# Attention's reciprocal row sums: to DRAM through a TensorE transpose, or straight from the 128x4 tile in 4-byte pieces

## The chip, the cores and the metric

The kernel runs on one core of a Trainium2 chip. The metric is the device time of one execution in microseconds (us); the time of a kernel is the median of its runs. Beside the times there is one profiled execution, from which all views are taken. A core has five engines that run their own instruction streams and wait for each other by semaphores: TensorE (PE, matrix multiply; its weight loads are shown apart as PEld), VectorE (DVE), ScalarE (ACT), GpSimd (POOL) and SyncE (SP). In this kernel SP issues every DMA, in the order of its own stream. SBUF is the on-chip memory with 128 partitions, PSUM holds TensorE's results in 8 banks, and DRAM is the chip's main memory.

## The reference

One inference step of a two-layer encoder, for a prompt of 1024 tokens and 8 samples of 16 tokens (1152 rows of width 1024), all in 4-byte floats. Each layer is attention with 16 heads of width 64, then a gated feed-forward network of width 2816 with a short causal convolution; each half is closed by a layer norm. Layer 0 attends to the own chunk of 64 and the 2 chunks before it, with a learned sink in the softmax; layer 1 to the own chunk and the 8 before it. What matters here is the softmax:

```
s = q . k * scale + bias           # per head, masked to the band
m = max(s)                         # layer 0: max(s.max, sink)
e = exp(s - m)
p = e / (e.sum + exp(sink - m))    # layer 1: p = e / e.sum
o = p . v
```

The division by the row sum can be made on `p` or, after the second product, on `o`; the kernel does it on `o`.

## The kernel before, in words

The stages follow each other: projections of the modulation vectors (`ada`), attention of layer 0 ("A" here), its output projection, feed-forward, attention of layer 1 ("B"), its output projection, feed-forward. Matmuls are run in split precision: each operand is a high and a low part, held in two tiles, and three products are added. The modulation weights of later stages are streamed in and multiplied in the background of attention A (`ada`, L209 loads and L211 matmuls).

Inside an attention, `work` is a list of 64 pairs: 8 column blocks `c` (two heads each), 2 heads `a`, 4 groups `g` of 256 queries. For each pair, in this order, there are

- `scores` (L507, L510 matmuls, softmax at L473 on DVE and L477 on ACT): unnormalised exponentials `p` with queries on the partitions, and their row sum into one column of the tile `L`, one column for each 128 queries; in A the row's maximum goes to `M`;
- `weigh`, one pair later: TensorE transposes of `p` (L533), evacuated by ACT and DVE (L538, L539);
- `values`, three pairs later in A and two in B: the second product (L552) and its evacuation into `on` (L563, L564), with head width on the partitions and queries along the row.

After every second pair, `sums` takes the four new columns of `L`: 128 partitions (queries) by 4 (query tiles). In A it adds the sink (L573, L574). It takes reciprocals (L575). The factor is needed along the row, for all 64 partitions of a head, since `on` has its queries there. So the four columns are turned into four rows by a TensorE transpose into a PSUM bank (L577, from the two banks `tbk` that `weigh` uses too), DVE copies them to the tile `rl` (L578), and a DMA writes 4 rows of 128 numbers, 512 bytes each, to the DRAM array `rD` (L580). When the values of both pairs are there, `normalise` reads the 512 numbers back with one DMA that repeats them on 64 partitions (L586, into `rb`), multiplies `on` by them (L589, on POOL, the very last one on DVE), and stores the result to DRAM (`oN`, L591), from where it is loaded for the output projection (`oload`, L597). The last column block stays in SBUF. `rb` has one place for each of the two heads `a`.

Beside this, small items handle the samples; they end in stores of 128 partitions by 4 by 16 numbers into `oSD` in B (L695). Loads of keys and values for the next head pair are at L436 and L437, of the bias at L485, of weights at L166, of the output projection's rows and constants at L806, L807, L811 and L907.

The Python order is a draft. A scheduler runs through it with estimated durations and decides the final order of every engine's stream, SP's DMAs among them; a change of one step moves others. Semaphores are derived from what reads and writes what; DMAs share eight completion semaphores in turn, so that a DMA also waits for the one that used its semaphore before.

Of the kernel before, what the change touches and what calls it, by code (L numbers as in the profile page):

```python
# [88 lines left out]
class Trunk:  # L89
# [249 lines left out]
    def attention(self, l, wk):  # L339
        nc, I = self.nc, self.I  # L340
# [32 lines left out]
        sa, sc = (fa, fa) if l == 0 else (Arena(self.adaT[:, 0:720]), Arena(self.cT))  # L373
        pTs = sa.take(384)
        osm = sc.take(128)
        rl = sc.take(128)
        L = sa.take(128)
        M = sa.take(128) if l == 0 else None
        ost = sa.ring(1, 512) if l == 0 else sa.ring(2, 64)
# [2 lines left out]
        tbk = Ring(TB[l])  # L382
# [35 lines left out]
        for p in range(2):  # L418
            t = sb.next()[:, 0:KS]
# [148 lines left out]
        def sums(x):  # L568

            hh = 2 * x.head.c + x.head.a  # L570
            cs = slice(hh * 8 + 2 * x.g - 2, hh * 8 + 2 * x.g + 2)
            if l == 0:
                nc.scalar.activation(M[:, cs], M[:, cs], AF.Exp, bias=self.sinkH[:, hh : hh + 1])  # L573
                nc.vector.tensor_add(L[:, cs], L[:, cs], M[:, cs])  # L574
            nc.vector.reciprocal(L[:, cs], L[:, cs])  # L575
            t = self.bank(tbk.next())
            nc.tensor.transpose(t[0:4, 0:128], L[:, cs], self.ident)  # L577
            nc.vector.tensor_copy(rl[0:4, :], t[0:4, 0:128])  # L578
            q0 = (x.g // 2) * 512
            nc.sync.dma_start(self.rD[l][hh, q0 : q0 + 512].rearrange("(g q) -> g q", q=128), rl[0:4, :])  # L580

        def normalise(c, a, h):
            r = slice(64 * a, 64 * a + 64)
# [145 lines left out]
        for i, x in enumerate(work):  # L729
            scores(x)  # L730
            if i and work[i - 1].g % 2:
                sums(work[i - 1])
            for c, bi in QAT.get(i, ()):
                if bi is None:
                    qload(c)
                else:
                    qblock(c, bi, qw[c])
            if i >= lw:
                weigh(work[i - lw])
            if i >= lag:  # L740
                finish(i - lag)
            self.step(BGA)
            if not self.bg and len(sbk.items) == 4:
                sbk.items = [0, 1, 2, 3, 4]
            for _ in range(ITEMS.count(i)):
                steps += items.pop(0)
            for _ in range(min(len(steps), 1 + (len(steps) > 4) + (len(steps) > 8))):
                steps.pop(0)()
            for c in OAT.get(i, ()):
                oload(c)  # L750
        assert not items
        for f in steps:
            f()
        sums(work[-1])
        for i in range(len(work) - lw, len(work)):
            weigh(work[i])
# [582 lines left out]
```

## Time and profile before

| | us |
|---|---|
| median of 3 runs | 2995.66 |
| lowest and highest | 2993.42, 2997.04 |
| the profiled execution | 2989.15 |
| its span, first to last instruction | 2987.3 |

The mean granted TensorE clock of the profiled execution is 0.984 of full speed. Attention A takes about 120 to 410 us of the span, attention B about 1665 to 2012 us, by the first and last instruction of `sums`. In the views, a group's row gives line, engine, operation, tiles and shapes, count, then busy time and mean length of one in ns, then the idle time of the engine before them and what ended it. "PE PS L577" means an instruction of line 577 on PE that writes PSUM. PEq, SPq and the like are the engines' sequencers, which issue DMAs and wait for semaphores. Lines are those of the kernel before.

### The profile page before, as it was taken

What the parts mean: (1) busy time and instruction counts of PE and PEld (TensorE: products, weight loads), DVE (VectorE), ACT (ScalarE), POOL (GpSimd) and SP (SyncE); (2) the same over time, 40 slices, a digit from 0 to 9 for tenths busy, and PEclk for the clock granted to TensorE, in tenths of its full rate; (3) what the DMA queues carried; (4) which work ended last, traced back from release to release, by engine and by line L of the source; (5) the groups of instructions that cost most, each with busy time, mean ns of one, the idle gap of its engine ahead of it and who ended that gap; (6) DMA issues with size and microseconds to landing.
All of it is one profiled execution on the core that took longest, in us unless ns stands there. A gap on an engine that the chain in (4) does not pass through costs nothing.

```text
span 2987.3 us, 43224 instructions
## 1 busy us (share of the span) xinstructions
PE 2863.8 (96%) x16582; PEld 2545.5 (85%) x16582; DVE 1537.3 (51%) x3416; ACT 1145.7 (38%) x2432; POOL 908.0 (30%) x661
## 2 busy tenths in 40 slices
PE   7999889999999999999999999989999999999996
PEld 4886668888888898997999888867899999999995
DVE  4365668424444343358412677766724444444468
ACT  3464643332222222224434666662442222222224
POOL 2122332322222222344561121231432222222253
PEclk9999989999999999999999999999999999999998
DMA  8655353722222222212795467673311111111121
GB/s 299 189 150 160 109 151 113 238 81 77 94 81 86 83 72 99 82 64 103 267 309 165 130 152 195 181 226 118 125 50 38 41 43 46 43 41 40 42 84 74
DMA packets 175535, 353.95 MB, mean 118 GB/s; under 512 B 34632, under 2 KB 91784, under 8 KB 174944
## 3 DMA queue, kind: packets, MB, share of 16 engines
q1 hardware_dynamic: 175328, 351.19, 37.0%
q8 instruction: 130, 2.13, 0.3%
q14 instruction: 77, 0.63, 0.1%
HBM read 285.22 MB, written 75.35 MB: 121 GB/s over the span
## 4 chain that ended last, share of the span: by engine, by line
PE 79%; DVE 8%; DMA 6%; ACT 3%; POOL 2%; issue 2%; SPq 0%; DVEq 0%; ACTq 0%; POOLq 0%
PE PS L267 46%; PE PS L1050 16%; PE PS L279 8%; PE PS L552 2%; PE PS L211 2%; PE PS L533 2%; DMA ws<-in_wo_dram 1%; PE PS L507 1%; DMA F<-in_adaw_dram 1%; DVE F L473 1%; PE PS L510 1%; DMA F<-xd 1%; DVE acc L1110 1%; DMA ws<-oN 1%; POOL wl L162 1%
## 5 line engine op out<-in xcount | busy, mean ns | idle before, releaser
L267 PE MATMUL PS<-H,wh 128*128 128x384 f32 (+1 forms) x5472 | 1045.9, 339 | 0.3 <-DVE H L162 0.3
L267 PEld LDWEIGHTS PS<-H,wh 128*128 128x128 f32 x5472 | 966.6, 188 | 17.5 <-issue 7.5
L162 POOL TENSOR_TENSOR wl<-ws,wh 128x1024 fp32r<-128x1024 f32 x167 | 404.8, 2429 | 751.1 <-ACT wh L151 704.0
L979 DVE SCALAR_TENSOR_TENSOR F<-PS,F 128x256 f32<-128x256 f32 (+2 forms) x704 | 352.9, 512 | 535.7 <-ACT F L976 522.5
L267 PE MATMUL PS<-H,wl 128*128 128x384 f32 (+1 forms) x2736 | 565.1, 343 | 19.6 <-POOL wl L162 7.8
L267 PEld LDWEIGHTS PS<-H,wl 128*128 128x128 f32 x2736 | 486.3, 189 | 53.2 <-issue 18.6
L976 ACT ACTIVATE F<-PS,F 128x384 f32<-128x384 f32 x264 | 177.3, 672 | 751.1 <-PE PS L267 749.6
L1050 PE MATMUL PS<-wh,X 128*128 128x512 f32 x1320 | 412.2, 394 | 10.3 <-DVE acc L1041 4.1
L1041 DVE TENSOR_TENSOR acc<-acc,PS 128x512 f32<-128x512 f32 x324 | 221.4, 685 | 271.6 <-PE PS L1050 271.1
L1025 POOL TENSOR_TENSOR F<-F 128x384 f32<-128x384 f32 x132 | 138.0, 1046 | 649.4 <-ACT F L1023 647.5
L1050 PEld LDWEIGHTS PS<-wh,X 128*128 128x128 f32 x1320 | 245.4, 188 | 64.0 <-issue 6.7
L151 ACT CAST wh<-ws 128x1024 fp32r<-128x1024 f32 x174 | 180.0, 1045 | 154.9 <-PE PS L1050 75.3
L1050 PE MATMUL PS<-wl,X 128*128 128x512 f32 x660 | 216.4, 392 | 0.0
L279 PE MATMUL PS<-wh,H 128*128 128x256 f32 (+1 forms) x936 | 172.5, 314 | 6.3 <-DVE H L162 6.0
L279 PEld LDWEIGHTS PS<-wh,H 128*128 128x128 f32 x936 | 137.3, 195 | 17.0 <-DVE H L162 6.8
L1050 PEld LDWEIGHTS PS<-wl,X 128*128 128x128 f32 x660 | 124.1, 188 | 28.1
L589 POOL TENSOR_TENSOR F<-F,x2att 64x512 f32<-64x512 f32 x62 | 79.4, 1280 | 212.8 <-DVE F L564 171.4
L162 DVE TENSOR_TENSOR X<-F,X 128x384 fp32r<-128x384 f32 x110 | 96.9, 881 | 88.7 <-ACT X L151 88.4
L279 PE MATMUL PS<-x1att,H 128*128 128x512 f32 x504 | 131.8, 402 | 4.9 <-ACT x1att L151 2.7
L533 PE MATMUL PS<-C,F 128*128 128x128 f32 x720 | 118.3, 285 | 17.4 <-DVE wh L539 7.5
L1023 ACT ACTIVATE F<-F 128x384 f32<-128x384 f32 x132 | 69.2, 524 | 143.3 <-DVE F L979 129.0
L279 PEld LDWEIGHTS PS<-x1att,H 128*128 128x128 f32 x504 | 94.7, 190 | 27.8 <-ACT x1att L151 3.4
(211 smaller groups left out, 3477.8 us busy)
## 6 DMA issues: line engine op xcount, KB each, us to landing
ws<-in_wup_dram SPq DMA_DIRECT2D x88, 512.0 KB
F<-in_adaw_dram SPq DMA_DIRECT2D x74, 512.0 KB
ws<-in_wdn_dram SPq DMA_DIRECT2D x44, 512.0 KB
ws<-in_adaw_dram SPq DMA_DIRECT2D x32, 512.0 KB
x1att<-kH SPq DMA_DIRECT2D x60, 256.0 KB
xd<-F SPq DMA_DIRECT2D x27, 512.0 KB
F<-xd SPq DMA_DIRECT2D x27, 512.0 KB
vH<-X SPq DMA_DIRECT2D x40, 256.0 KB
```

What stands on the lines that cost most here:

```text
L151: nc.scalar.copy(out, in_)
L162: self.eng(el).tensor_sub(lo, src, hi.bitcast(F32))
L267: self.nc.tensor.matmul(out[:, 0:n], w[a][:, k * 128 : k * 128 + 128], H[:, p, k, s0 : s0 + n], start=i == 0, stop=i == 23)
L279: self.nc.tensor.matmul(out[:, 0:n], H[:, p, j * kn + k, t0 : t0 + 128], w[a][:, k * n : k * n + n], start=i == 0, stop=i == 23,)
L533: nc.tensor.transpose(t[:, m * 128 : m * 128 + 128], p[:, (kt - k0) * 128 : (kt - k0) * 128 + 128], self.ident)
L589: self.eng("v" if last else "p").tensor_mul(on[r, q], on[r, q], rb[r, :])
L976: nc.scalar.activation(y, ps[:, off : off + 384], AF.Identity, bias=w(3), scale=w(2))
L979: nc.vector.scalar_tensor_tensor(o, u, w(i), o, op0=ALU.mult, op1=ALU.add)
L1023: nc.scalar.activation(y, y, AF.Gelu_apprx_tanh)
L1025: nc.gpsimd.tensor_mul(a, y, ya[bi])
L1041: nc.vector.tensor_add(row[:, n], row[:, n], ps)
L1050: nc.tensor.matmul(ps, ac[m][p][:, cs], w[m][q][:, n], start=i == 0, stop=i == 5)
```

## The change

The transpose, the PSUM bank and the copy are gone, and with them the tile `rl`. The DMA reads the 128x4 tile as it stands and writes each number to its place: from partition `q` four numbers, 512 bytes apart in DRAM. The contents of `rD` are the same, and its reader is unchanged. In A, the tiles that were laid out behind `rl` (`L`, `M`, `ost`) move down by 128 columns.

```diff
         osm = sc.take(128)
-        rl = sc.take(128)
         L = sa.take(128)
...
             nc.vector.reciprocal(L[:, cs], L[:, cs])
-            t = self.bank(tbk.next())
-            nc.tensor.transpose(t[0:4, 0:128], L[:, cs], self.ident)
-            nc.vector.tensor_copy(rl[0:4, :], t[0:4, 0:128])
             q0 = (x.g // 2) * 512
-            nc.sync.dma_start(self.rD[l][hh, q0 : q0 + 512].rearrange("(g q) -> g q", q=128), rl[0:4, :])
+            nc.sync.dma_start(self.rD[l][hh, q0 : q0 + 512].rearrange("(g q) -> q g", q=128), L[:, cs])
```

## The prediction

> **What bounds the kernel now.** I read the page's engine shares first, then the two attention stages as windows, then the waits inside them, and last the timeline around one row-sum step. The page's first part and two windows (columns: length, then busy time and instruction count of each engine, granted clock, DMA share, GB/s):
>
> ```profile
> PE 2863.8 (96%) x16582; PEld 2545.5 (85%) x16582; DVE 1537.3 (51%) x3416; ACT 1145.7 (38%) x2432; POOL 908.0 (30%) x661
> 120.00:410.00 290.00, 266.54 (x1908) 210.42 (x1907) 188.06 (x652) 173.81 (x521) 89.90 (x84) 0.94 0.46 139
> 1665.00:2012.00 347.00, 326.89 (x2525) 280.39 (x2524) 248.23 (x804) 229.35 (x558) 81.74 (x75) 1.00 0.66 178
> ```
>
> The kernel is TensorE's: 96% of the span. The change lives in two stages, attention A (120 to 410 us, 290 us long) and attention B (1665 to 2012 us, 347 us long), together 637 us. There PE is busy 92% and 94%, so it idles 23.5 and 20.1 us; DVE is busy 65% and 72%, DMA 46% and 66%. A TensorE instruction taken away here should nearly all come off the end, and nothing that is gained can be much larger than the removed slots and those 44 us of idle time. The next two views show the instructions that go, and one whole step in order of time (start, length, engine, line):
>
> ```profile
> L577 PE MATMUL PS<-C,F 128*4 128x128 f32 x32 | 8.8, 276 | 1.0 <-DVE F L692 0.5 <-DVE X L539 0.3
> L577 PE MATMUL PS<-C 128*4 128x128 f32 x32 | 8.7, 272 | 0.3 <-DVE C L692 0.2
> L578 DVE COPY F<-PS 4x128 f32<-4x128 f32 x32 | 8.8, 276 | 14.8 <-PE PS L577 14.5
> L578 DVE COPY C<-PS 4x128 f32<-4x128 f32 x32 | 8.8, 275 | 13.2 <-PE PS L577 11.8 <-DMA rD<-C 1.3
> ```
>
> ```profile
> 1703.65 0.17 DVE L575 RECIPROCAL C<-C 128x4 f32<-128x4 f32 x1
> ...
> 1711.40 0.27 PE L577 MATMUL PS<-C 128*4 128x128 f32 x1
> ...
> 1711.43 0.39 PE L507 MATMUL PS<-x1att 128*128 128x320 f32 x1
> ...
> 1711.71 0.28 DVE L578 COPY C<-PS 4x128 f32<-4x128 f32 x1 [2.05 <-PE PS L577]
> ...
> 1712.06 0.43 SPq L580 DMA_DIRECT2D rD<-C  x1
> ...
> 1715.83 0.45 SPq L586 DMA_DIRECT2D x2att<-rD  x1
> ```
>
> The reciprocal ends at 1703.82, the transpose starts 7.6 us later, the copy ends at 1711.99, the row goes to DRAM at 1712.06, and its reader is issued at 1715.83. So the detour over PE costs this step 8.2 us of latency, although its two instructions work for 0.55 us; DVE stands 2.05 us before the copy.
>
> **The change, part by part.** *The 64 transposes (32 in each stage).* What one takes of PE's stream is the distance between starts, not its 0.27 us:
>
> ```profile
> 2008.56 0.27 PE L577 MATMUL PS<-C 128*4 128x128 f32 x1
> 2008.67 0.27 PE L683 MATMUL PS<-C 128*128 128x128 f32 x1
> ```
>
> Here it is 0.11 us; in the block above the next matmul starts 0.03 us behind it. The full 0.27 us would be a slot in which nothing overlaps. Bounds 64 x 0.03 = 2 and 64 x 0.27 = 17 us; I take 64 x 0.11 = **-7.0 us**, since most neighbours are small matmuls like that of 2008.67. PE's idle time just before them is 1.0 + 0.3 = 1.3 us; some of it will only move to the next instruction: **-1 us** with bounds 0 and -1.3.
>
> *The 64 copies* free 8.8 + 8.8 = 17.6 us of DVE, and 14.8 + 13.2 = 28 us in which DVE stood in front of them, holding what was queued behind: the evacuations of scores and transposed weights. Those are what PE waits for in B:
>
> ```profile
> PE PS L533 <- DVE X L539: 5.8, 10, 1.3
> PE PS L533 <- DVE wh L539: 5.2, 5, 2.2
> PE PS L533 <- DVE C L578: 0.6, 2, 0.3
> ```
>
> These are 11.6 us of the 20.1. DVE loses 17.6 + 28 = 45.6 of 637 us, 7%, but its next instruction often waits for PE or ACT too. I take a sixth of the 11.6, **-2 us**, with bounds 0 and -6 (half). The copy's bank of the pair that transposes share also falls away, which is the 0.6 us row.
>
> *The write.* It now waits for the reciprocal alone. SP's side of it (who waited, us in total, times, longest):
>
> ```profile
> SPq L580 <- DVE F L578: 62.1, 22, 9.3
> SPq L586 <- DMA rD<-C: 48.0, 27, 7.4
> SPq L580 <- DVE C L578: 26.6, 12, 6.0
> SPq L586 <- DMA rD<-F: 15.7, 10, 3.3
> ```
>
> SP stood 62.1 + 26.6 = 88.7 us for the copy; most of that goes, since the reciprocal is done earlier by what the block above shows. SP stood 48.0 + 15.7 = 63.7 us in front of the reader until the write had landed, 1.7 us in each of 37 waits, and this can grow. Instead of 4 rows of 512 bytes there are 512 pieces of 4 bytes. The nearest thing in the trace is the store of the sample rows, also 512 pieces from 128 partitions into DRAM, of 64 bytes each. Issue times, and the DMA view of 2010.3 to 2011.9 us, which holds one of these stores and nearly nothing else:
>
> ```profile
> L580 SPq DMA_DIRECT2D rD<-C x32: 257/352/479, 1668.7 to 2009.2; - x32
> L695 SPq DMA_DIRECT2D oSD<-C x16: 359/377/578, 1802.7 to 2013.0; - x16
> DMA packets 529, 0.03 MB, mean 21 GB/s; under 512 B 529, under 2 KB 529, under 8 KB 529
> q1 hardware_dynamic: 529, 0.03, 20.9%
> ```
>
> To issue it costs SP 0.025 us more (377 against 352). On the DMA engines it is 20.9% of 1.6 us = 0.33 us, so 64 of them add 21 us to 637, some 3 points of a share of 46 and 66%. The pieces are a sixteenth of those, so 0.33 us is rather high for moving them; what the memory makes of 4-byte writes no row shows. I bound the extra landing by 0 and by a doubling of the mean wait, 1.7 us, and take 0.33 us. With the write issued several us earlier this is covered in mid-stage; I charge **+1 us** for where it isn't (bounds 0, and the rival below).
>
> The Trainium skill ("DMA: Bandwidth & Descriptors", Rules for kernel authors) speaks against this edit: a last dimension that isn't contiguous becomes one descriptor per element and should be rearranged. The packet row agrees on the count (512 pieces and their completion marks, 529 packets); the price, 0.33 us, is the row's.
>
> *Moved instructions.* The scheduler writes a new order for every engine. Comparing the two built orders: in A, a row's reader stands about 10 places behind its write in SP's queue (median of 32), before about 4; in B it stays at about 2. So in B each reader still waits for its write, with key, value and weight loads queued behind, and PE behind those. In A's tail, the last output weight now goes ahead of the gate and norm rows (L806 to L811):
>
> ```profile
> 413.95 0.93 SPq L811 DMA_DIRECT2D F<-in_ln_dram  x2
> 415.28 0.33 SPq L166 DMA_DIRECT2D ws<-in_wo_dram  x1
> 430.57 0.74 PE L279 MATMUL PS<-x1att,H 128*128 128x512 f32 x2 [1.54 <-ACT x1att L151]
> ```
>
> The weight shared the engines with those rows and PE stood 1.54 us for what it had to pass through: **-1 us**, bounds 0 and -1.5; the gate rows land later instead. In B's tail only the sample rows' reload moves behind one norm row, which I cost at nothing: the wait there is for the store, issued before both.
>
> The sum: -7 - 1 - 2 + 1 - 1 = **-10 us**.
>
> **Rivals.**
> *The slots were not PE's bound.* If ACT and DVE set PE's pace, the transposes ran in gaps: only the 2 us of the 0.03 us bound and 1 us of waits come off. For it: 11.6 us of PE's waits in B end with DVE. Against: PE is 94% busy there. -3 us, 2993.
>
> *SP's queue is held (slower).* The landing wait lasts longer than the transfer, since each 4-byte piece must be confirmed by DRAM, and SP, which issues in order, holds the loads behind the reader. In mid-stage loads run ahead, but at the end of each attention they don't:
>
> ```profile
> 320.00:360.00 40.00, 34.19 (x273) 26.10 (x271) 29.41 (x102) 28.44 (x86) 18.23 (x16) 0.97 0.44 127
> 1945.00:1985.00 40.00, 34.25 (x323) 24.85 (x321) 29.50 (x105) 27.17 (x66) 15.45 (x11) 1.00 0.92 267
> ```
>
> PE idles 5.8 of 40 us in each of these, and the DMA engines are 92% busy in the second. Some 20 of the writes lie in 320 to 410 and 1905 to 2012 us (32 x 90/290 and 32 x 107/347, 10 each). If an extra e on each of them comes through in full, it cancels the gain from e = 10/20 = 0.5 us on. Midway between 0.33 and 1.7 us, e = 1.0 us: -10 + 20 = +10 us, 3006; at 1.7 us it is -10 + 34 = +24, 3020. For it: the 7.4 us that one write already took. Against: writes start earlier than before. The skill's page (Specifications) has a rule that points here: below 512 bytes a transfer is a read-modify-write. The 64-byte pieces fall under it as well, and their 0.33 us contains no such penalty on the engines.
>
> *A new order costs one more slow stretch in A.* From 240 to 280 us PE was short of ada weights and its clock fell:
>
> ```profile
> 240.00:280.00 40.00, 34.33 (x236) 23.73 (x234) 23.04 (x87) 20.45 (x65) 8.03 (x10) 0.83 0.61 178
> PE PS L211 <- DMA ws<-in_adaw_dram: 4.0, 4, 1.8
> ```
>
> That stretch lost 5.7 us of idle time and 17% of 34.3 = 5.8 us of clock. A second one eats the gain: -10 + 11.5 = +1.5, 2997. For it: every queue in A is rewritten. Against: the same rewriting may as well remove the first one.
>
> **The numbers.** The profiled execution took 2989.15 us, its span 2987.3 and 1.85 around it; the median of three runs is 2995.66, 6.5 us above, and I predict against the median. My forecast is 2995.66 - 10 = 2986, chance 0.46; slots not PE's bound 0.16 (2993); SP's queue held 0.28 (3006); one more slow stretch 0.10 (2997). A change of this kernel shows from about 0.2%, 6 us, on: the three runs span 3.6. Faster by more 0.46; within it 0.16 and half of 0.10, 0.21; slower 0.28 and the other half, 0.33. The low end adds the far bounds, -7 - 1.3 - 6 - 1.5 = -16, and the slow stretch gone, some -6: 2974. The high end lies in the held queue, short of its 1.7 us bound: 3015. The forecast's own range is 2978 to 2990 (-18 to -6).
>
> **What would show it.** Right: no L577 and L578; packets under 512 bytes up by some 33,000; PE busy in the two stages down together by about 7 us with idle time no longer than 44 us; the reader's wait for the write at 64 to 85 us in all. The held queue: that wait above 64 + 64 x 0.5 = 96 us, with PE's idle time grown at 320 to 410 and 1905 to 2012. The third: a 40 us window in A with a clock under 0.85 that has none now. Wrong altogether: a change of time outside the two stages and their tails, or rows' writes that add much more than 0.33 us each to the DMA share.

## The result, and the profile after

The forecast was 2986 us with a range of 2974 to 3015. Measured were 3311.62 us (median of 6 runs, 3298.04 to 3319.05), against 2994.54 us for the kernel before (6 runs, 2990.44 to 3000.43). The ratio is 1.105 with a 95% interval of 1.1031 to 1.1069: 317 us slower, far outside the range. The profiled execution after took 3315.62 us, span 3313.8; its span is 326.5 us longer than that of before. The mean granted clock is 0.932 (before 0.984). From the place of `rl` on, line numbers of the kernel after are lower by 1, and behind the removed transpose by 4: the write is L576, its reader L582, the multiplication L585, the store `oN` L587, the `ada` matmul L211 as before.

The page's engine shares and its DMA part, and then the DMA part of before:

```profile
PE 2923.5 (88%) x16518; PEld 2592.2 (78%) x16518; DVE 1528.1 (46%) x3352; ACT 1148.0 (35%) x2432; POOL 908.0 (27%) x661
DMA packets 208814, 353.95 MB, mean 107 GB/s; under 512 B 68168, under 2 KB 125064, under 8 KB 208224
```

```profile
DMA packets 175535, 353.95 MB, mean 118 GB/s; under 512 B 34632, under 2 KB 91784, under 8 KB 174944
```

PE has 64 instructions fewer and is busy 59.7 us longer than its 2863.8 of before. The rest of the 326.5 us is idle time of PE: 3313.8 - 2923.5 = 390.3 us, against 2987.3 - 2863.8 = 123.5. The bytes moved are the same to 0.01 MB; the packets under 512 bytes rose from 34632 to 68168, by 33,536. The next view is the span after in five stretches (length, busy time and count of PE, PEld, DVE, ACT, POOL, then granted clock, DMA share, GB/s); the second is attention A, the fourth attention B:

```profile
0.00:117.00 117.00, 97.61 (x545) 76.00 (x546) 41.43 (x87) 33.46 (x68) 27.24 (x33) 0.93 0.80 272
117.00:540.00 423.00, 282.49 (x1785) 219.35 (x1783) 179.02 (x604) 168.27 (x511) 79.73 (x78) 0.78 0.55 89
540.00:1825.00 1285.00, 1243.62 (x6840) 1118.66 (x6841) 569.28 (x1032) 414.90 (x775) 418.95 (x272) 0.98 0.38 127
1825.00:2330.00 505.00, 357.34 (x2497) 308.53 (x2497) 242.75 (x775) 231.96 (x559) 81.46 (x75) 0.82 0.61 123
2330.00:3313.00 983.00, 942.43 (x4858) 869.62 (x4856) 495.57 (x857) 299.45 (x521) 300.64 (x203) 0.98 0.18 60
```

Attention A takes 423 us where it took some 290, attention B 505 where it took 347. So most of the loss, 130 us in A (117 to 540 against 117 to 410 us) and 158 in B, is where the changed writes are. A has lost some background work as well: the stretch after it has 6840 PE instructions against 6736 in the like stretch of before (410 to 1665 us). In A and B the clock is 0.78 and 0.82 (before 0.94 and 1.00) and PE idles 141 and 148 us (before 23.5 and 20.1). The bandwidth fell from 139 to 89 and from 178 to 123 GB/s while the DMA engines' busy share went from 0.46 to 0.55 and from 0.66 to 0.61: busy engines that move little. PE's longest waits, first in A, then in B, and those of SP over the whole span (us in total, times, longest):

```profile
PE PS L211 <- DMA ws<-in_adaw_dram: 86.9, 13, 16.3
```

```profile
PE PS L666 <- DMA F<-in_cvB_dram: 57.3, 7, 14.2
PE PS L532 <- DVE wl L538: 18.9, 1, 18.9
PE PS L509 <- DMA x1att<-kH: 17.1, 3, 13.2
```

```profile
SPq L582 <- DMA rD<-C: 154.6, 21, 11.4
SPq L587 <- POOL F L585: 145.8, 28, 11.3
SPq L582 <- DMA rD<-F: 61.2, 9, 9.9
```

In A, PE waits 86.9 us for the modulation weights, for which it waited 4.0 us before; in B for samples' values and for keys. None of those tiles has to do with the row sums. The reader (L582) stands 154.6 + 61.2 = 215.8 us in front of writes that have not landed, 7.2 us in each of 30 waits; before it was 63.7 us in 37. A first step of A in order of time on SP (start, length), and the DMA view of 118 to 134 us in slices of 0.4 us (busy share of the engines in tenths, then GB/s):

```profile
117.94 0.38 SPq L576 DMA_DIRECT2D rD<-F  x1
118.43 0.44 SPq L166 DMA_DIRECT2D ws<-in_wq_dram  x1
128.57 0.45 SPq L582 DMA_DIRECT2D x2att<-rD  x1
129.13 0.53 SPq L484 DMA_DIRECT2D F<-ska  x1
```

```profile
DMA  0068799000001990798990654460231489771000
GB/s 0 0 5 82 82 143 20 0 0 0 0 0 51 92 41 10 20 31 41 20 41 0 31 20 10 31 31 10 20 31 20 164 246 225 164 248 51 20 8 0
```

The 2 KB write is issued at 117.94, a 512 KB weight load right behind it. The reader, which waits for the write, is issued at 128.57: the write took 10.3 us from the end of its issue. In that time only it and the weight load have been issued, yet after a first 1.6 us the load's bytes stop for 2 us and then come, but for one slice, at 0 to 51 GB/s. From the 32nd slice on (130.4 us), with the write landed and the reader and L484's load issued, 164 to 248 GB/s are moved. The engines look busy at 20 GB/s because the load's 4 KB packets are stretched: one takes 0.159 us in the median of attention A before, and up to 10 us here. The write's own 4-byte packets all start within 0.9 us of the end of its issue, are recorded as 7 to 9 ns each, and don't show what goes on.

Measured in this way for all 64 writes (end of issue to the last completion event in the trace), the landing took 0.89 us at least and 1.78 us in the median before, 8.83 and 11.00 after. Over all writes of the after trace, the other DMA traffic ran at 175 and 188 GB/s in the first two us behind an issue, at 132 and 101 in the next two, at 37 to 52 from the sixth to the eleventh, and was back at 160 in the fourteenth; behind the writes of before it ran at 141 to 183 in all fourteen. In A such a write is issued every 13 us ((537.8 - 117.9)/32), in B every 16: for six of these 13 to 16 us the loads run at a third or less of the 160 GB/s.

So two theories were to be told apart. One is the rival of the prediction: SP, in order, stands before the reader, and what is queued behind it comes late. The other: the write holds the core's whole DMA, whoever waits for it. The second then has to say what in the write does it: 512 pieces, 4 bytes, or where they go.

### The profile page after: what moved, and what is told of

Read it like the earlier page. It is cut to its first block, busy times and chain, and to the rows that moved or that the text cites. A ratio compares the mean times of both kernels' runs of the same rounds, so it can differ in the third digit from the quotient of the medians.

```text
span 3313.8 us, 42982 instructions
## 1 busy us (share of the span) xinstructions
PE 2923.5 (88%) x16518; PEld 2592.2 (78%) x16518; DVE 1528.1 (46%) x3352; ACT 1148.0 (35%) x2432; POOL 908.0 (27%) x661
## 2 busy tenths in 40 slices
DMA packets 208814, 353.95 MB, mean 107 GB/s; under 512 B 68168, under 2 KB 125064, under 8 KB 208224
## 5 line engine op out<-in xcount | busy, mean ns | idle before, releaser
L267 PE MATMUL PS<-H,wl 128*128 128x384 f32 (+1 forms) x2736 | 573.5, 346 | 20.0 <-POOL wl L162 9.4
L267 PEld LDWEIGHTS PS<-H,wl 128*128 128x128 f32 x2736 | 494.2, 192 | 56.5 <-issue 16.9
L532 PE MATMUL PS<-C,F 128*128 128x128 f32 x720 | 131.5, 305 | 34.7 <-DVE wl L538 19.2
L585 POOL TENSOR_TENSOR F<-F,x2att 64x512 f32<-64x512 f32 x62 | 79.1, 1275 | 282.2 <-DVE F L563 111.2
L472 DVE CUSTOM_DVE_ANT_0 F<-PS,F,C 128x256 f32<-128x256 f32 (+3 forms) x208 | 96.9, 479 | 93.4 <-PE PS L509 44.7
L532 PEld LDWEIGHTS PS<-C,F 128*128 128x128 f32 x720 | 94.3, 155 | 53.2 <-DVE wl L538 20.0
```

The source lines that it names most:

```text
L267: self.nc.tensor.matmul(out[:, 0:n], w[a][:, k * 128 : k * 128 + 128], H[:, p, k, s0 : s0 + n], start=i == 0, stop=i == 23)
L472: nc.vector.tensor_tensor_reduce(out=p[:, c0 : c0 + w], in0=ps, in1=b, scale=1.0, scalar=init, op0=ALU.add, op1=ALU.min, accum_out=nm)
L532: nc.tensor.transpose(t[:, m * 128 : m * 128 + 128], p[:, (kt - k0) * 128 : (kt - k0) * 128 + 128], self.ident)
L585: self.eng("v" if last else "p").tensor_mul(on[r, q], on[r, q], rb[r, :])
```

## Experiments on who is held

*The reader taken off the write.* The change stays; the reader loads from an input that is always there.

```diff
-            src = self.rD[l][2 * c + a : 2 * c + a + 1, q]
+            src = self.I["ln"][0:1, q]
```

> The changed kernel, but the factors are read from an input in DRAM that nobody writes, so that nothing waits for the 4-byte writes (the reciprocals are left out of the result). T1: the engines are held as before, 3200 to 3310. T2: the wait is gone, 2985 to 3010. T3: about 3300.

Measured: 3227.05 us, ratio 1.0779 (1.0755 to 1.0803), 236 us over the kernel before (differences of medians here and below). PE's two longest waits, over the whole span:

```profile
PE PS L211 <- DMA ws<-in_adaw_dram: 74.8, 13, 12.1
PE PS L666 <- DMA F<-in_cvB_dram: 34.8, 6, 11.9
```

The reader no longer waits for the write. What is left is 29.7 us in all that SP waits for these writes before other DMAs (completion semaphores are shared), against 215.8. And 236 of 317 us, 74%, are still there, in the same waits. Taking the reader off brought 81 us, with whatever its new order of instructions does; so much can be put down to the held queue.

*The write alone.* The kernel before with all its parts, and one write more: the same 512 pieces, to an array that nobody reads.

```diff
             nc.sync.dma_start(self.rD[l][hh, q0 : q0 + 512].rearrange("(g q) -> g q", q=128), rl[0:4, :])
+            nc.sync.dma_start(self.rX[l][hh, q0 : q0 + 512].rearrange("(g q) -> q g", q=128), L[:, cs])
```

> The kernel before, whole, and beside its own write one of 512 pieces of 4 bytes into a DRAM array that nobody reads. T1: 64 holds, +200 to +320 us, 3200 to 3310, and the other transfers' landings grow. T2: nobody waits for it but the eighth DMA behind it, which shares its semaphore: under +20, 3015. T3: the order stays near that of before, 2995 to 3010.

Measured: 3278.24 us, 1.095 (1.0921 to 1.0979), +287 us. One wait of PE in A (117 to 520 us), and the GB/s of 117.5 to 133.5 us, again in slices of 0.4 us, around a first such write:

```profile
PE PS L212 <- DMA ws<-in_adaw_dram: 64.0, 15, 11.8
```

```profile
GB/s 0 0 0 4 32 123 164 10 0 0 0 0 0 143 20 20 41 20 51 10 41 31 31 10 20 20 10 51 10 105 321 298 77 8 10 92 266 220 297 389
```

The same ditch of low GB/s, of about the same length (8.4 against 9.6 us), with the transposes, the copies and an order near that of before all in place. The write as such is enough for a loss of 287 us; neither the removal of work nor the new order is needed for it. Its landing here was 7.21 us at least, 10.41 in the median.

This run does not separate the two theories, though nobody reads the new write. The kernel's own write of 4 rows is caught too: its landing went from 1.78 to 7.43 us in the median, and its reader and the next copy into `rl` wait for it, over the whole span:

```profile
SPq L588 <- DMA rD<-C: 163.4, 29, 10.9
DVE C L579 <- DMA rD<-C: 93.2, 14, 17.7
PE PS L534 <- DVE C L579: 58.2, 15, 12.8
```

It is the run without the reader that tells them apart. The hold is not one of SP's queue alone, either. Another queue (q8, "instruction" in the page) has 130 packets of 16 KB in each execution. The longest of them takes 1.72 us in the kernel before. In the changed kernel nine take 2.5 to 4.4 us, and with the extra write nine take 2.1 to 3.6, all of them in attentions A and B.

*The removed work alone.* The changed kernel with the write of before (4 rows of 512 bytes), taken from a constant tile; the factors are not in it.

```diff
-            nc.sync.dma_start(self.rD[l][hh, q0 : q0 + 512].rearrange("(g q) -> q g", q=128), L[:, cs])
+            nc.sync.dma_start(self.rD[l][hh, q0 : q0 + 512].rearrange("(g q) -> g q", q=128), self.ident[0:4, :])
```

> The transposes and copies are left out, and the write takes 4 rows of 512 bytes from a constant tile in place of the row sums, so the factors are left out of the result: it prices the removed PE and DVE work alone, with the write of before. T1 and T2: my forecast of -10 us for these terms, 2985 (2977 to 2990). T3: most of +317 stays, above 3200.

Measured: 3002.63 us, 1.0031 (1.002 to 1.0042). The expectation was missed, and the reason lies in the experiment. Its writes:

```profile
L576 SPq DMA_DIRECT2D rD<-C x64: 239/293/478, 28.8 to 69.1; - x64
```

As they depend on nothing, the scheduler put all 64 into the prologue, and A's scores started 16 us later than before (126.3 against 110.2). It shows that without 4-byte pieces the 317 us are gone, but it gives no price of the removed work.

## Experiments on what in the write does it

*The same write in pieces of 16 bytes.* Each partition's four numbers lie side by side in DRAM: 128 pieces of 16 bytes. The reader is unchanged, and the multiplication reads its factors in the permuted order.

```diff
-            nc.sync.dma_start(self.rD[l][hh, q0 : q0 + 512].rearrange("(g q) -> q g", q=128), L[:, cs])
+            nc.sync.dma_start(self.rD[l][hh, q0 : q0 + 512].rearrange("(q g) -> q g", g=4), L[:, cs])
...
-            self.eng("v" if last else "p").tensor_mul(on[r, q], on[r, q], rb[r, :])
+            o3 = on[r, q].rearrange("p (g q) -> p g q", q=128)
+            self.eng("v" if last else "p").tensor_mul(o3, o3, rb[r, :].rearrange("p (q g) -> p g q", g=4))
```

> The transposes and copies stay away, but each partition now writes its four numbers as one piece of 16 bytes (128 pieces to consecutive addresses instead of 512 of 4 bytes), and the multiplication reads the factors in the order in which they then lie. Three theories of the +317 us of the changed kernel (3311.6 against 2994.5): T1, each 4-byte write leaves all DMA engines nearly without throughput for about 8 us, whoever waits; T2, the engines are free and only SP stands for the late landing, with the loads queued behind it; T3, the scheduler's new order is bad. T1: the hold goes with the pieces; if it goes with their number, a quarter of +317 (about 3065), if only pieces of 4 bytes are held, 2985. T2: the landing falls to 1.4 us as that of the 64-byte store, 2985. T3: the order is nearly that of the changed kernel, so above 3250.

Measured: 2999.24 us, 1.0024 (1.0009 to 1.0038). The 317 us are gone, although the transposes are gone as well. That it is 8 us slower than before, not faster, is taken up below.

*The extra write in other forms.* All of these are the kernel before with one write more to an array that nobody reads. First: the same 512 pieces, each in 64 bytes of its own; half as many pieces of 4 bytes; 256 pieces of 8 bytes; and 512 pieces of 4 bytes into SBUF.

```diff
+            nc.sync.dma_start(   # pieces 64 bytes apart
+                self.rX[l][hh, 16 * q0 : 16 * q0 + 8192].rearrange("(g q s) -> q g s", q=128, s=16)[:, :, 0], L[:, cs]
+            )
...
+            nc.sync.dma_start(   # half of the pieces
+                self.rX[l][hh, q0 : q0 + 256].rearrange("(g q) -> q g", q=128), L[:, cs.start : cs.start + 2]
+            )
...
+            nc.sync.dma_start(   # 8 bytes
+                self.rX[l][hh, q0 : q0 + 512].rearrange("(j q e) -> q j e", j=2, e=2),
+                L[:, cs].rearrange("q (j e) -> q j e", e=2),
+            )
...
+            nc.sync.dma_start(self.xs.next().rearrange("p (g s) -> p g s", s=2)[:, :, 0], L[:, cs])   # SBUF
```

> As the run with an extra write (the kernel before plus 512 pieces of 4 bytes into an array that nobody reads, +285 us), but the pieces go 64 bytes apart, so that no two share a 64-byte line. If the hold goes with the number of small pieces: +285 again, 3200 to 3310. If it comes from pieces that meet in the same line (16 in each line in the extra write): under +30, 2990 to 3020.

> As the extra write, but only two of the four columns: 256 pieces of 4 bytes, over half the lines. If the hold goes with the number of pieces, each write holds the engines 4 to 5 us and the time grows by +90 to +140, 3080 to 3135. If the pieces of one line wait for each other while the lines work side by side, it stays near +285, 3230 to 3290.

> As the extra write, but 256 pieces of 8 bytes, the same 2 KB. If the number of pieces decides: like the half write, 3080 to 3135. If the pieces of one line (8 here, 16 before) decide: the hold halves too, so it is read against the half write, where a line still has 16. If only pieces of 4 bytes are held: under +20, 2990 to 3010.

> As the extra write, 512 pieces of 4 bytes, but into SBUF (the same partitions, 8 bytes apart), not into DRAM. If DRAM's handling of small writes makes the hold: under +20, 2990 to 3010. If the DMA engines are slow with 4-byte pieces wherever they go: +285, 3200 to 3310.

After these four, two more, to see the way between a pitch of 4 and one of 64 bytes:

```diff
+            nc.sync.dma_start(   # pieces 8 bytes apart
+                self.rX[l][hh, 2 * q0 : 2 * q0 + 1024].rearrange("(g q s) -> q g s", q=128, s=2)[:, :, 0], L[:, cs]
+            )
...
+            nc.sync.dma_start(   # pieces 16 bytes apart
+                self.rX[l][hh, 4 * q0 : 4 * q0 + 2048].rearrange("(g q s) -> q g s", q=128, s=4)[:, :, 0], L[:, cs]
+            )
```

> As the extra write, 512 pieces of 4 bytes, but 8 bytes apart: 8 pieces in each 64-byte line, as in the write of 8-byte pieces, which took +60 us (ratio 1.0214) with half the pieces. If the pieces in a line decide, and not their size: well under the +285 of 16 in a line, with a shortest landing of 2.5 to 5 us; 64 lines instead of 32 may double the +60: 3050 to 3115. If pieces of 4 bytes in a shared line are held whatever their number: +200 or more, above 3190.

> The same, 16 bytes apart: 4 pieces in each 64-byte line, as in the write of 16-byte pieces, whose shortest landing was 1.06 us. If the pieces in a line decide: +5 to +30, 2995 to 3020, and a shortest landing under 2.5 us. If any sharing of a line by 4-byte pieces is held: above 3100.

All six and the first extra write, each against the kernel before in its own comparison; "per 64 bytes" counts how many pieces start in the same 64 bytes of DRAM:

| extra write | per 64 bytes | ratio (95%) | us more | landing, least / median us |
|---|---|---|---|---|
| 512 x 4 B, 4 apart | 16 | 1.095 (1.0921-1.0979) | 287 | 7.21 / 10.41 |
| 256 x 4 B, 4 apart | 16 | 1.0788 (1.0757-1.082) | 232 | 6.39 / 8.98 |
| 512 x 4 B, 8 apart | 8 | 1.0208 (1.0167-1.0249) | 63 | 2.82 / 5.01 |
| 256 x 8 B, 8 apart | 8 | 1.0214 (1.0184-1.0243) | 61 | 2.48 / 4.77 |
| 512 x 4 B, 16 apart | 4 | 1.0079 (1.0063-1.0095) | 22 | 2.01 / 3.65 |
| 512 x 4 B, 64 apart | 1 | 1.0038 (0.9996-1.008) | 13 | 1.39 / 2.62 |
| 512 x 4 B into SBUF | - | 1.0032 (1.0013-1.0051) | 9 | 1.34 / 2.61 |

Two expectations were missed: half of the pieces, at 3222 us, lay between the two forecasts (3080 to 3135 if the number decides, 3230 to 3290 if pieces in a common 64 bytes wait for each other) and near the second; the 8-byte pieces, at 3050 us, lay below the forecast by the number (3080 to 3135) and above that by the size (2990 to 3010).

The number of pieces does not decide: 512 of them cost from 13 to 287 us, and half of them 232, where a price per piece would give 143. Nor does their size: 256 pieces of 8 bytes and 512 of 4 at the same pitch cost nearly the same, 61 and 63 us. Nor does the stretch of DRAM that a write covers: the first row and the 8-byte row cover the same 2 KB and cost 287 and 61 us. What goes with the cost is how closely the pieces lie in DRAM, and much steeper than in proportion: from 4 to 8 bytes apart the cost falls to about a fifth, and at 64 bytes it can't be told from that of a write into SBUF. The 9 to 13 us of the last two rows, of which the 13 is not clear of zero, are then what 64 more transfers of 512 pieces cost that meet no such thing. The contrast to the ditch, in the same place of A, with the pieces 64 bytes apart: SP's issues, PE's wait in A (117 to 420 us), and the GB/s of 121.5 to 137.5 us in slices of 0.4 us:

```profile
121.50 0.38 SPq L582 DMA_DIRECT2D rX<-F  x1
121.99 0.44 SPq L167 DMA_DIRECT2D ws<-in_wq_dram  x1
```

```profile
PE PS L212 <- DMA ws<-in_adaw_dram: 6.1, 5, 1.9
```

```profile
GB/s 0 0 5 52 41 174 195 348 358 133 10 0 5 0 41 36 210 77 5 72 266 133 297 369 420 318 389 369 259 63 1 0 51 205 399 389 261 10 1 4
```

The same weight load stands behind the write and comes at up to 358 GB/s; PE's wait for the modulation weights is back at 6.1 us, from 64.0, and the longest packet of q8 in the whole execution takes 1.91 us.

What is not settled is what the memory does with such neighbours. That 64 bytes are the unit is an assumption of the table's column: the runs vary the distance, not the alignment. In all these writes, too, neighbours in DRAM come from neighbouring partitions, and no run takes many close pieces from one partition.

## Experiments on the version that keeps the gain

With 16-byte pieces A's last scores ended 10 us earlier than before (377.2 against 387.3 us), yet the first transposes of the layer norm behind A came 7 us later (456.3 against 449.0). SP's order at A's end, and one link of the chain of waits in 405 to 470 us:

```profile
409.04 0.45 SPq L582 DMA_DIRECT2D x2att<-rD  x1
409.54 0.58 SPq L803 DMA_DIRECT2D F<-gd  x1
410.17 0.68 SPq L804 DMA_DIRECT2D F<-gd  x1
...
411.44 0.38 SPq L166 DMA_DIRECT2D ws<-in_wo_dram  x1
...
412.34 0.65 SPq L927 DMA_DIRECT2D F<-oSD  x1
```

```profile
412.34 12.99 DMA F<-oSD
```

The reload of the sample rows, with which the output projection begins, was put behind gate rows, norm rows and a weight, and took 12.99 us to land. In the kernel before it was issued ahead of these:

```profile
411.54 0.37 SPq L930 DMA_DIRECT2D F<-oSD  x1
412.01 0.53 SPq L586 DMA_DIRECT2D x2att<-rD  x1
412.59 0.58 SPq L806 DMA_DIRECT2D F<-gd  x1
```

There it landed 4.74 us after the end of its issue, with 16-byte pieces 12.34 us after. So the remedy was to state the order, for both kernels: the reload first, then the constants.

```diff
-        with self.tc.issue_after(self.lastdma):
+        s3 = self.xring.next().rearrange("p (c t) -> p c t", t=128)
+        ld = nc.sync.dma_start(s3, self.oSD.rearrange("c p t -> p c t"))
+        with self.tc.issue_after(ld.ins):
             self.ln_consts(l, 0)
...
             if t == 8:
-                s3 = self.xring.next().rearrange("p (c t) -> p c t", t=128)
-                nc.sync.dma_start(s3, self.oSD.rearrange("c p t -> p c t"))
```

On the kernel before:

> The kernel before with one change of order: at the end of each attention the gate and norm rows (2 MB) are loaded behind the reload of the sample rows, not ahead of it. PE waits for that reload: 4.4 us in B before; in the run with 16-byte pieces, where 2.5 MB stood ahead of it, the reload took 13 us in A. If the order of this tail decides: 3 to 8 us less than before, 2985. If the gate rows, now later, become the wait: no change or +3.

And on that with 16-byte pieces:

> The run with 16-byte pieces (no transposes, no copies, +7 us against before) with the same change of order. If my forecast of the removed PE and DVE work (-10 us) was right and the lost tail of A ate it: 12 to 18 us less than with 16-byte pieces alone, 2981 to 2987, and some 5 us under the run with the order alone. If the removed work is worth nothing: the same time as the run with the order alone.

Measured: 2989.22 us on the kernel before, 0.9993 (0.9984 to 1.0002), no difference; 2981.49 us with 16-byte pieces, 0.9964 (0.9951 to 0.9976), 10.7 us faster than the kernel before and the lowest median of all. SP's order at A's end in the latter:

```profile
412.59 0.45 SPq L582 DMA_DIRECT2D x2att<-rD  x1
414.01 0.38 SPq L920 DMA_DIRECT2D F<-oSD  x1
414.48 0.74 SPq L803 DMA_DIRECT2D F<-gd  x1
```

The reload now landed 3.74 us after the end of its issue, and the first transposes of the layer norm came at 446.5 us, ten us earlier than without the remedy (446.8 in the kernel before with the same tail).

The engine shares of the page, first of the kernel before with this tail, then of the 16-byte pieces with it:

```profile
PE 2867.6 (96%) x16582; PEld 2551.3 (85%) x16582; DVE 1534.2 (51%) x3416; ACT 1145.5 (38%) x2432; POOL 902.8 (30%) x661
```

```profile
PE 2857.3 (96%) x16518; PEld 2548.3 (85%) x16518; DVE 1527.8 (51%) x3352; ACT 1146.8 (38%) x2432; POOL 926.4 (31%) x661
```

Between these two, which differ by the change alone (in its 16-byte form), lie 2989.22 - 2981.49 = 7.7 us, with intervals that do not meet, and 10.3 us of PE's busy time in the profiled executions. That is what the change is worth once the write is harmless. That it comes from the 64 transposes and copies is argued from PE's busy time; the two profiled executions lie only 1.5 us apart (2986.71 and 2985.21) and can't show where the 7.7 us are. POOL's multiplications with permuted factors are 23.6 us longer (926.4 against 902.8) and cost nothing that the end shows.

## Why the prediction was wrong

*The failed step is the price of the write.* It was put at 0.33 us on the engines and +1 us in all, from the nearest row, the store of the samples: also 512 pieces from 128 partitions, of 64 bytes. That row agreed in the number of pieces and in being small, and differed in what decides: its pieces have 64 bytes of DRAM each to themselves. At that distance 64 extra writes cost 13 us, 0.2 us each and not clear of zero, which fits the row's 0.33 us; at a distance of 4 bytes they cost 287 us, 4.5 us each. The upper bound, a doubling of the mean wait by 1.7 us, had no row behind it: the median landing grew by 9.2 us. What the prediction wrote beside it, "what the memory makes of 4-byte writes no row shows", was true, and no bound could be had from these rows; the range had to say so and did not. The low end was added up wrongly besides: it is said to hold the far bounds, but takes the slots at -7, whose far bound was -17 (2964 instead of 2974), and the forecast's own -18 stands in no sum. Neither changes the outcome.

*The held queue.* The sign was that rival's, and its mark was there, 215.8 us of the reader's wait where over 96 was named. But most of the mechanism was another. The rival let the delay reach PE through SP, which stands before the reader, and only at the two ends, in some 20 writes; so its price ended at +24 us. The runs show that the core's other transfers are slowed while the write lasts, in mid-stage too and with the reader off the write, and taking it off brought 81 of 317 us. The argument "against", that writes start earlier, does not help against a hold of this kind.

*The third rival* named a clock under 0.85 in a new stretch of A. Two such stretches were there before, not one: 240 to 280 us at 0.83, and 360 to 400 at 0.82, which the prediction overlooked. After, of the ten 40-us stretches from 120 to 520 us all but three have one, down to this:

```profile
480.00:520.00 40.00, 26.06 (x178) 18.55 (x178) 19.58 (x68) 14.20 (x44) 16.63 (x15) 0.59 0.30 61
```

It comes with PE's waits, and with an order near that of before too (with the extra write PE is busy 2946.4 us), so the new order is not needed for it. In the two stages PE is busy 46 us longer, 282.49 + 357.34 against 266.54 + 326.89, with 151 instructions fewer, where -7 was forecast.

*Number and size of the pieces.* The prediction took the number of pieces as given and priced them by the 64-byte row; but the number is not what costs. The Trainium skill ("DMA: Bandwidth & Descriptors", Rules for kernel authors) advised against the form of this write, one descriptor per element. The trace agrees on the count, with 33,536 more packets. The Trainium skill's other rule on the same page (Specifications), read-modify-write below 512 bytes, does not tell the cases apart: all of the extra writes fall under it, and those into DRAM cost from 13 to 287 us. It may be that pieces in a common stretch of memory have to be read and rewritten one after the other; no run here shows that.

*Of the "wrong altogether" marks* one came true as written: the DMA engines' busy time in the two stages rose from 0.46 x 290 + 0.66 x 347 = 362 us to 0.55 x 423 + 0.61 x 505 = 541, 2.8 us for each of the 64 writes, eight times 0.33.

*What held.* L577 and L578 with their bank and the 33,000 packets came as said. Slots and copies, -10 us with the waits, are -7.7 us by the pair with equal tails, nearer to the forecast than to the rival that gave them 3 us. The tail was the wrong way round: -1 us was booked in A for the last weight ahead of the gate rows, and the reload's place was costed at nothing, in B. With 16-byte pieces it was A's reload that moved, behind gate rows, norm rows and that weight, and it turned a gain of ten us at A's last scores into a loss of seven; with the reload put first the gain stayed.

## What to carry to other kernels

A DMA that scatters 4-byte pieces next to each other in DRAM was here not a slow small transfer but a brake on the core's other transfers; write each partition's numbers side by side, here 16 bytes, and let the consumer read them permuted. A nearest row prices a new transfer only if it agrees in what decides, and size and number of pieces are not all of that: where they lie belongs to it, and one extra write to an unread array, added to the kernel before, measures it in one run. When work that bounds the kernel has been removed and nothing is gained, look at the next tail for a load that the new order put last.

## What the runs showed of the hardware

- One 2 KB write in 4-byte pieces side by side took 8.83 us at least and 11.00 in the median to land, and the core's other DMA traffic ran at 37 to 52 GB/s for six of these us, against 160 thereafter. Packets of another queue were slowed as well: up to 4.4 us for 16 KB, against 1.72 at most before.
- The cost of 64 such writes by the pieces' distance: 287 us at 4 bytes, 63 at 8, 22 at 16, 13 at 64 (not clear of zero), as against 9 into SBUF; with half the pieces at 4 bytes it is 232.
- The packets of the write do not show it: in the step shown they are recorded as 7 to 9 ns each, and the time appears in the packets of other transfers, up to 10 us for one of 4 KB. The GB/s row beside the busy row shows it, and so do waits for tiles that have nothing to do with the write.
